# A pool of their own for the small statistics tiles: the same program at other SBUF addresses

## The chip, the cores and the metric

The kernel runs on one core of one Trainium2 chip. The metric is the device time of one execution in microseconds (us). A core has TensorE (PE), which multiplies; VectorE (DVE) and ScalarE (ACT), which work element by element; GpSimd (POOL); SyncE (SP), which here issues nearly all transfers; and DMA engines, which move data between HBM and the on-chip memory, SBUF. A tile in SBUF takes the same byte addresses in each of 128 partitions; "address" below is the byte offset within a partition.

## What is computed

Two layers of a transformer-like trunk for one sequence of 256 tokens with 1,024 features, in fp32. Each layer is a SwiGLU FFN, a mixer, and another FFN, each behind an RMS norm that is modulated by a conditioning vector `c`:

```
mod = (silu(c) @ ada_w[i] + ada_b[i]).reshape(B, 3, 3, 1024)       # shift, scale, gate of each sublayer
pre(z, j) = rms_norm(z, norm_g[i, j]) * (1 + scale[j]) + shift[j]
x = x + 0.5 * gate[0] * swiglu_ffn(pre(x, 0), w_in[i, 0], w_out[i, 0])   # 1024 -> 2 x 2816 -> 1024
x = x + gate[1] * mixer(pre(x, 1))      # layer 0: causal attention, 16 heads; layer 1: convolution module
x = x + 0.5 * gate[2] * swiglu_ffn(pre(x, 2), w_in[i, 1], w_out[i, 1])
```

With 256 tokens the attention has one block, so it is plain causal attention with distance penalties and RMS norms of queries and keys. The convolution module is a pointwise product with a sigmoid gate, a depthwise convolution of width 31, a layer norm, swish and a second pointwise product.

## The kernel before

**Products in three passes.** To come near fp32 accuracy each operand is split into a high part and a low part (the rest), both in the type fp32r. `mm3` (L604) then issues three matmuls for each block: high x high (L606), high x low (L607), low x high (L608). In the trace's names `whi`, `wlo` are the parts of a weight, `hh`, `hl` those of the activations, `gh`, `gl` those of the FFN's hidden values. "u<-whi,hh" is a matmul into the PSUM tile `u` whose moving operand is `whi` (512 columns, 2,048 bytes) and whose stationary operand is 128 columns of `hh`.

**The stream of weights.** `plan` lists all weights in the order of use, in units of 1 MB. `issue` (L187) loads half a unit into one of six `raw` buffers of 4,096 bytes a partition, `high_part` (L229) copies it to `whi` on ScalarE (L241), `step` (L204) makes `wlo` on VectorE (L216). `whi` and `wlo` have six buffers each. Woven into the stream are parts of `ada_w`, which VectorE folds into an accumulator `acc` (`ada_fold`, L279) and TensorE sums over the partitions. The order of all instructions is written out by hand, and the feeding is tied to the products: before each block of products (`block`, L254) a set number of stream entries is taken.

**An FFN** (`ffn`, L641) goes over 11 blocks of 256 hidden columns. For each block and each of two token tiles `cols512` (L610) makes the up-projection into a bank `u` with `hh`/`hl` as stationary operands; `gate` makes `g` (L654, L655); `TR` (L678) transposes `g` (L684) and splits it into `gh` (ACT, L692) and `gl` (DVE, L693); `rows256` (L621), called by `Dn` (L695), makes the down-projection into two banks `y` with `gh`/`gl` as stationary operands. Attention and convolution use the same `rows256` for their last product, with `hh`/`hl` as stationary operands.

**Between sublayers** `residual` (L533) adds to `x`, `square` sums squares into `ss`, and `rms` (L557) makes `v` and `r` from it, one value for each token; `scaled` makes the normalised rows `z`, and `turn` transposes and modulates them (`hf`) into `hh`, `hl`.

**Where tiles lie.** SBUF is given out pool by pool in the order in which pools are opened, within a pool tag by tag as tiles are first asked for. A tile takes a multiple of 32 bytes and begins right behind the last one:

```
self.const = pool("const")
self.rawp = pool("rawp", RAW)
self.hlp = pool("hlp", RING)
self.keep = pool("keep")
self.two = pool("two", 2)
```

`const` holds tables of many sizes and ends at byte 21,088, which is 608 past a multiple of 2,048. `rawp`, `hlp` (`whi`, `wlo`) and `keep` (`x`, `hh`, `hl`) follow with tiles of whole multiples of 2,048 bytes, so all of these begin 608 past a multiple. In `two` the tiles `ss0`, `ss1`, `v0`, `r0`, `v1`, `r1` (4 or 8 bytes, two buffers each) stand between the large ones, so `sq` begins 736, `z` 864, `hf` 992 past a multiple. Each stage then opens a pool of its own (`f0`, `at`, `f1`, `cv`, `f3`) behind `two`: `g`, `gh`, `gl`, `ah`, `al` of the FFNs begin 992 past a multiple. `raw` lies at 21,088 and up, `whi` at 45,664, `wlo` at 94,816, `hh` at 152,160, `hl` at 160,352, `gh` at 203,744 and `gl` at 209,888 (three buffers each).

Of the kernel before, what the change touches and what calls it, by code (L numbers as in the profile page):

```python
# [8 lines left out]
F32 = mybir.dt.float32  # L9
# [25 lines left out]
class Unit:  # L35
    """One megabyte of weights, [128, 2048], as a high and a low part.

    parts: (sources, view of the unit that they fill) twice, half a megabyte each.
    """

# [6 lines left out]
class Vec:  # L47
    """A modulation vector: 0 shift, 1 scale, 2 gate."""

# [7 lines left out]
class Trunk:  # L57
    def __init__(self, ctx, tc, a):
        self.tc, self.nc, self.a = tc, tc.nc, a

        def pool(name, bufs=1, **kw):
            return ctx.enter_context(tc.tile_pool(name=name, bufs=bufs, **kw))

        self.const = pool("const")
        self.rawp = pool("rawp", RAW)
        self.hlp = pool("hlp", RING)
        self.keep = pool("keep")
        self.two = pool("two", 2)
        self.ps = pool("ps", 1, space=bass.MemoryType.PSUM)
        self.vecs = {(l, s, k): Vec(l, s, k) for l in range(2) for s in range(3) for k in range(3)}  # L70
        self.sums = []
        self.phase = 0
        self.ss, self.rs, self.zs = {}, {}, {}
        self.quota = self.credit = 0
        self.plan()

# [1 line left out]
    def plan(self):  # L78
# [3 lines left out]
        def pair_unit(w, c0, n, u):  # L82
            """columns c0.. and c0 + width.. (n of each) of 1024 / n k tiles"""
            nk = 1024 // n
# [5 lines left out]
        def early_unit(w, c0, u):  # L90
            """the same, but with half of the k tiles in each part"""
            rows = w[u * 512 : (u + 1) * 512, :].rearrange("(k p) n -> p k n", p=P)
            return Unit([
                ([rows[:, 2 * s : 2 * s + 2, c : c + 256] for c in (c0, c0 + DFF)], half(s)) for s in range(2)
            ])
# [4 lines left out]
        def col_unit(w, c0, u):  # L100
            """512 columns of four k tiles"""
            rows = w[u * 512 : (u + 1) * 512, c0 : c0 + 512].rearrange("(k p) n -> p k n", p=P)
            return Unit([([rows[:, 2 * s : 2 * s + 2, :]], half(s)) for s in range(2)])

        def row_unit(w, j):
            """all columns of two k tiles"""
            rows = w[j * 256 : (j + 1) * 256, :].rearrange("(k p) n -> p k n", p=P)
# [14 lines left out]
        def weave(main, entries, start):  # L122
            """main units, the entries spread evenly among them from unit number start on"""
            done = 0
# [60 lines left out]

# [1 line left out]
    def issue(self):  # L187
# [16 lines left out]
    def step(self, eng=None):  # L204
        """Take the next entry of the stream; False where it has to wait for a ring slot."""
        nc = self.nc
# [22 lines left out]
    def high_part(self, i):  # L229
        """The high part of entry i; False where it has to wait for a ring slot."""  # L230
        e = self.stream[i]
# [22 lines left out]
    def block(self):  # L254
        """Before a block of products: entries that the other engines can take meanwhile."""
        self.run_sums()
# [49 lines left out]
    def row_sum(self, vec, ah, al, c):  # L306
        """A gate's 512 columns, on all partitions."""
        nc = self.nc
# [6 lines left out]
    def column_sum(self, vec, acc, c):  # L315
        """Four blocks of a shift or a scale, features on the partitions."""
        nc = self.nc
# [5 lines left out]
    def finish(self, vec, src, c, n=4):  # L323
        """Adds the bias; a scale becomes norm_g * (1 + scale)."""
        nc = self.nc
# [9 lines left out]

# [1 line left out]
    def start(self):  # L337
# [53 lines left out]
        def idle(n):  # L391
            """keeps the tensor engine's clock up while it waits"""
            for _ in range(n):
# [5 lines left out]
        nc.tensor.transpose(pt[:, P : P + 72], ab[0], self.ident[:72, :72])  # L399
        self.ss[0] = self.two.tile([P, 2], F32, name="ss0", tag="ss0")  # L400
        self.ss[1] = self.two.tile([P, 2], F32, name="ss1", tag="ss1")
        up = self.p[0]["up"]
# [15 lines left out]
        def turn(q, fold):  # L418
            """The modulation of a quarter and its part of the stationary operand, among the splits."""
            fin = self.early_sum(q, *fold, idle)  # L420
# [23 lines left out]
        def lead(U):  # L444
            """Quarters of the features: their modulation, then three column blocks' products."""
            for q in range(4):
# [15 lines left out]
    def early_fold(self, q):  # L462
        """256 columns of the first scale and shift from four entries of the stream: the vector engine
        folds the scale's two and the shift's first."""
        nc = self.nc
# [21 lines left out]
    def early_sum(self, q, accs, last, idle):  # L487
        """The tensor engine adds the shift's second entry and sums the partitions."""
        nc = self.nc
# [17 lines left out]
    def early_transposes(self, q):  # L507
        """Two k tiles of the normalised rows, features on the partitions."""
        ps = self.bank("m")
# [7 lines left out]
    def early_turn(self, q, ps):  # L517
        """Their modulation; the function that it returns makes them a stationary operand."""
        nc = self.nc
# [11 lines left out]

# [1 line left out]
    def residual(self, t, y, gate, f, last=False):  # L533
        nc, x = self.nc, self.x[t]
        if not last:
            self.ss[t] = self.two.tile([P, 2], F32, name=f"ss{t}", tag=f"ss{t}")
        for o, n in ((0, 512), (512, 256), (768, 256)) if last else ((0, 512), (512, 512)):
# [19 lines left out]
    def rms(self, t, halves=(0, 1)):  # L557
        nc, ss = self.nc, self.ss[t]
        v = self.two.tile([P, 1], F32, name=f"v{t}", tag=f"v{t}")
        r = self.rs[t] = self.two.tile([P, 1], F32, name=f"r{t}", tag=f"r{t}")  # L560
        nc.vector.scalar_tensor_tensor(v, ss[:, 0:1], EPS * D, ss[:, 1:2], op0=ALU.add, op1=ALU.add)
# [4 lines left out]
    def scaled(self, t, h):  # L566
        """512 columns of the normalised rows"""
        z = self.zs[t, h] = self.two.tile([P, 512], F32, name="z", tag="z", bufs=3)
# [4 lines left out]
    def turn(self, t, l, s):  # L573
        """Transposes of the normalised rows, modulated, split into the stationary operand."""
        hf = [self.modulate(t, l, s, h) for h in range(2)]
# [26 lines left out]

# [1 line left out]
    def mm3(self, out, lh, ll, rh, rl, start, stop):  # L604
# [5 lines left out]
    def cols512(self, ps, t, unit, u):  # L610
        """ps [128 tok, 512] += h[t] @ the four k tiles of a unit"""
        self.need(unit)
# [8 lines left out]
    def rows256(self, y, lh, ll, unit, first, last, mid=None):  # L621
        """y (two halves) [128 tok, 1024] += the two k tiles of a unit; lh(k), ll(k): stationary;
        mid(): something to do between the halves"""
        self.need(unit)
# [14 lines left out]

# [1 line left out]
    def ffn(self, i, l, s, before, after, first=None, last=False, mid=None):  # L641
        """before(): turns the second token tile; after(): turns the first for the next sublayer;
        mid(): something to do on the way"""
        nc, p = self.nc, self.p[i]
# [97 lines left out]

# [1 line left out]
    def attention_constants(self):  # L744
        """dist[p, j] = 128 + p - j, or a large number where the key comes after the query. The scores
        are taken over minus the head's slope, so that all heads add the same distances; gqk[., pair]
        carries that and 1 / sqrt(64)."""
        nc = self.nc
# [167 lines left out]

# [1 line left out]
    def taps(self):  # L918
        """w2[32 q + c, r, b] = tap 4 r + q of channel 32 b + c, 0 for tap 31"""
        nc = self.nc  # L920
# [21 lines left out]
    def conv(self, cp, before, after):  # L942
# [35 lines left out]
        def UT(ps, b, t):  # L978
            """ps [128 tok, 256]: both halves of a unit's columns for one token tile"""
            unit = self.pw1[b]  # L980
# [13 lines left out]
        def across(b, t, e, c):  # L994
            """a unit's columns back into the form of U"""
            if b not in us:
# [15 lines left out]
        def spread(b):  # L1012
            """R[32 j + c, g, n] = u[32 g + c, n + j]"""
            u = ub[b % 3]
# [144 lines left out]

# [1 line left out]
    def run(self):  # L1161
# [52 lines left out]
```

## Time and profile before

| | |
|---|---|
| time, median of 3 runs | 1077.59 us (1076.84 to 1079.13) |
| span of the profiled execution, first to last instruction | 1075.8 us |
| what lies around the span, against the median | 1.8 us |
| PE / DVE / ACT busy share of the span | 97% / 76% / 47% |
| granted TensorE clock, mean | 0.984 |
| moved by DMA | 250.26 MB, 233 GB/s in the mean |

The page gives the busy time of each engine, the chain of work that ended last, the costliest groups of instructions and the transfers. A matmul's recorded length is longer than the distance to the next one's start, since matmuls overlap; so the distance of starts is what a product costs, and the recorded length is used to compare alike products. The stages lie at about 0 to 205 us (first FFN), 205 to 375 (attention), 375 to 548 (second FFN), 548 to 722 (third), 722 to 890 (convolution), 890 to 1076 (fourth).

### The profile page before, as it was taken

To read this page: it belongs to the slowest core of one execution; us is meant where nothing else is said; L and a number is where in the kernel's file an instruction comes from. 1 tells how busy PE (TensorE), PEld (TensorE's weight loads), DVE (VectorE), ACT (ScalarE), POOL (GpSimd) and SP (SyncE) were. 2 spreads that over 40 slices of the span, in tenths; PEclk is the share of its full clock that TensorE was granted. 3 is DMA by queue.
4 is the path that set the end of the run, shared out by engine and by line. 5 is a ranking of instruction groups with operands and counts; after the bars stand their busy time and mean duration, and the time that the engine had idled before them with its cause. 6 is when DMAs were issued, how large, how long until landed. Compare 5 with 4: busy or idle time off the path is not lost.

```text
span 1075.8 us, 14807 instructions
## 1 busy us (share of the span) xinstructions
PE 1043.1 (97%) x5522; PEld 853.2 (79%) x5522; DVE 815.4 (76%) x1267; ACT 503.9 (47%) x794; POOL 53.0 (5%) x83
## 2 busy tenths in 40 slices
PE   8999999999999999999999999999988799999998
PEld 7888788877777788888878888888867588888886
DVE  5878878879997798778478788776789768556643
ACT  3354344555676544444354444454545446434420
POOL 3000000001210000000020000000211100000000
PEclk8999999999999999999999999999989899999999
DMA  9979999948766399898739889885646127775711
GB/s 301 295 246 337 300 324 300 328 157 272 235 217 214 115 313 314 282 307 288 240 101 309 287 287 316 283 281 156 172 149 208 61 75 240 262 230 194 232 40 39
DMA packets 181692, 250.26 MB, mean 233 GB/s; under 512 B 8389, under 2 KB 132070, under 8 KB 181620
## 3 DMA queue, kind: packets, MB, share of 16 engines
q1 hardware_dynamic: 180784, 248.55, 70.0%
q0 software_dynamic: 688, 0.71, 0.3%
q8 instruction: 43, 0.70, 0.3%
q14 instruction: 29, 0.24, 0.1%
q10 hardware_dynamic: 148, 0.06, 0.0%
HBM read 248.24 MB, written 1.05 MB: 232 GB/s over the span
## 4 chain that ended last, share of the span: by engine, by line
PE 85%; DVE 9%; issue 2%; DMA 1%; ACT 1%; POOL 1%; SPq 0%; DVEq 0%; POOLq 0%; ACTq 0%
PE u L606 14%; PE u L608 14%; PE u L607 14%; PE y L606 11%; PE y L608 11%; PE y L607 11%; DVE R L1022 3%; DVE wlo L216 2%; PE m L684 2%; PE m L320 1%; DMA raw<-in_ada_w_dram 1%; PE m L497 1%; PE m L1031 1%; DVE x L543 1%; PE m L585 1%
## 5 line engine op out<-in xcount | busy, mean ns | idle before, releaser
L241 ACT ACTIVATE whi<-raw 128x1024 fp32r<-128x1024 f32 x320 | 328.8, 1055 | 167.8 <-DMA raw<-in_ffn_w_in_dram 101.7
L216 DVE TENSOR_TENSOR wlo<-raw,whi 128x1024 fp32r<-128x1024 f32 x320 | 382.5, 1224 | 32.7 <-ACT whi L241 32.6
L606 PE MATMUL u<-whi,hh 128*128 128x512 f32 x672 | 266.5, 397 | 0.0
L608 PE MATMUL u<-whi,hl 128*128 128x512 f32 x672 | 262.8, 391 | 0.0
L607 PE MATMUL u<-wlo,hh 128*128 128x512 f32 x672 | 261.9, 390 | 0.0
L279 DVE SCALAR_TENSOR_TENSOR acc<-raw,sc,acc 128x512 f32<-128x512 f32 x224 | 169.6, 757 | 5.3 <-DMA raw<-in_ada_w_dram 0.4
L608 PEld LDWEIGHTS u<-whi,hl 128*128 128x128 f32 x672 | 126.1, 188 | 28.3 <-DVE hl L601 1.2
L606 PEld LDWEIGHTS u<-whi,hh 128*128 128x128 f32 x672 | 126.3, 188 | 25.7 <-ACT hh L600 0.7
L607 PEld LDWEIGHTS u<-wlo,hh 128*128 128x128 f32 x672 | 126.3, 188 | 25.3
L606 PE MATMUL y<-whi,gh 128*128 128x512 f32 x352 | 140.6, 400 | 0.2 <-ACT gh L692 0.2
L608 PE MATMUL y<-whi,gl 128*128 128x512 f32 x352 | 139.0, 395 | 0.0
L607 PE MATMUL y<-wlo,gh 128*128 128x512 f32 x352 | 138.9, 395 | 0.0
L693 DVE TENSOR_TENSOR gl<-m,gh 128x512 fp32r<-128x512 f32 (+1 forms) x48 | 31.1, 647 | 96.2 <-ACT gh L692 96.0
L606 PE MATMUL y<-whi,hh 128*128 128x512 f32 (+1 forms) x256 | 97.9, 383 | 0.0
L608 PE MATMUL y<-whi,hl 128*128 128x512 f32 (+1 forms) x256 | 95.2, 372 | 0.0
L607 PE MATMUL y<-wlo,hh 128*128 128x512 f32 (+1 forms) x256 | 94.8, 370 | 0.0
L692 ACT ACTIVATE gh<-m 128x512 fp32r<-128x512 f32 (+1 forms) x48 | 26.9, 561 | 135.4 <-PE m L684 135.3
L654 ACT ACTIVATE sg<-u 128x256 f32<-128x256 f32 x84 | 32.2, 383 | 113.3 <-PE u L608 112.3
L608 PEld LDWEIGHTS y<-whi,gl 128*128 128x128 f32 x352 | 66.3, 188 | 16.1 <-DVE gl L693 0.4
L606 PEld LDWEIGHTS y<-whi,gh 128*128 128x128 f32 x352 | 66.3, 188 | 15.2 <-ACT gh L692 0.7
L607 PEld LDWEIGHTS y<-wlo,gh 128*128 128x128 f32 x352 | 66.5, 189 | 14.7
L655 DVE TENSOR_TENSOR g<-u,sg 128x256 f32<-128x256 f32 x84 | 35.5, 422 | 35.0 <-ACT sg L654 34.6
(157 smaller groups left out, 981.0 us busy)
## 6 DMA issues: line engine op xcount, KB each, us to landing
raw<-in_ffn_w_in_dram SPq DMA_DIRECT2D x164, 512.0 KB, 5.2
raw<-in_ada_w_dram SPq DMA_DIRECT2D x144, 512.0 KB, 5.1
raw<-in_ffn_w_out_dram SPq DMA_DIRECT2D x88, 512.0 KB, 5.3
raw<-in_attn_w_qkv_dram SPq DMA_DIRECT2D x24, 512.0 KB, 5.1
raw<-in_conv_w_pw_dram SPq DMA_DIRECT2D x24, 512.0 KB, 5.4
raw<-in_ffn_w_in_dram SPq DMA_DIRECT2D x24, 256.0 KB, 5.5
raw<-in_attn_w_o_dram SPq DMA_DIRECT2D x8, 512.0 KB, 4.4
gate<-in_ada_b_dram SPq DMA_DIRECT2D x6, 512.0 KB, 7.0
```

Of the source, the lines that this page charges most:

```text
L216: (eng or nc.vector).tensor_tensor(lo, raw, hi.bitcast(F32), op=ALU.subtract)
L241: self.nc.scalar.activation(hi, self.like(self.raws[i], hi), AF.Copy)
L279: nc.vector.scalar_tensor_tensor(dst, raw[:, i, :], self.sc[:, k : k + 1], dst, op0=ALU.mult, op1=ALU.add)
L606: nc.tensor.matmul(out, lh, rh, start=start, stop=False)
L607: nc.tensor.matmul(out, lh, rl, start=False, stop=False)
L608: nc.tensor.matmul(out, ll, rh, start=False, stop=stop)
L654: nc.scalar.activation(sg, ps[:, 0:256], AF.Silu)
L655: nc.vector.tensor_tensor(gs[c][:, t, :], ps[:, 256:512], sg, op=ALU.mult)
L684: nc.tensor.transpose(ps[:, o : o + P], g[:, t, k * P : k * P + P], self.ident)
L692: nc.scalar.activation(hi, src, AF.Copy)
L693: nc.vector.tensor_tensor(lo, src, hi.bitcast(F32), op=ALU.subtract)
L1022: nc.vector.tensor_copy(dst, src)
```

## The change

The tiles `ss0`, `ss1`, `v0`, `v1`, `r0`, `r1` get a pool of their own, `tiny`, behind `const`, and a pool with one tile of 264 floats, which nothing reads or writes, fills the bytes up to the next multiple of 2,048. (Comments and docstrings were emptied as well, which moves line numbers by two and nothing else.)

```
         self.const = pool("const")
+        self.tiny = pool("tiny", 2)
+        pool("pad").tile([P, 264], F32, name="pad")
         self.rawp = pool("rawp", RAW)
...
-        self.ss[0] = self.two.tile([P, 2], F32, name="ss0", tag="ss0")
-        self.ss[1] = self.two.tile([P, 2], F32, name="ss1", tag="ss1")
+        self.ss[0] = self.tiny.tile([P, 2], F32, name="ss0", tag="ss0")
+        self.ss[1] = self.tiny.tile([P, 2], F32, name="ss1", tag="ss1")
...
-            self.ss[t] = self.two.tile([P, 2], F32, name=f"ss{t}", tag=f"ss{t}")
+            self.ss[t] = self.tiny.tile([P, 2], F32, name=f"ss{t}", tag=f"ss{t}")
...
-        v = self.two.tile([P, 1], F32, name=f"v{t}", tag=f"v{t}")
-        r = self.rs[t] = self.two.tile([P, 1], F32, name=f"r{t}", tag=f"r{t}")
+        v = self.tiny.tile([P, 1], F32, name=f"v{t}", tag=f"v{t}")
+        r = self.rs[t] = self.tiny.tile([P, 1], F32, name=f"r{t}", tag=f"r{t}")
```

The instructions, their order and the semaphores on which they wait are the same on every engine. What differs is where tiles begin, in bytes past a multiple of 2,048:

| tiles | before | after |
|---|---|---|
| `raw`, `whi`, `wlo`, `x`, `hh`, `hl` | 608 | 0 |
| `sq` | 736 | 0 |
| `z` | 864 | 0 |
| `hf`, the gates, `tmp` | 992 | 0 |
| FFN pools: `g`, `gh`, `gl`, `acc`, `ah`, `al` | 992 | 0 |
| attention pool: `acc`, `vt`, `qT`, `kT` | 1,120 | 128 |
| attention pool: `p` (three buffers of 1,536 bytes) | 1,120, 608, 96 | 128, 1,664, 1,152 |
| convolution pool: `acc`, `b2`, `wd` | 512 | 1,568 |
| convolution pool: `R` (two buffers) | 512, 960 | 1,568, 2,016 |
| `ident`, `ones` and the rest of `const` | as they are | the same |

Behind `const` everything lies 1,056 to 1,440 bytes higher: `hh` at 153,600, `gh` at 204,800.

## Rows read from the trace of the kernel before

**Rows 1.** The page: busy times, and the chain's shares by engine.

```profile
PE 1043.1 (97%) x5522; PEld 853.2 (79%) x5522; DVE 815.4 (76%) x1267; ACT 503.9 (47%) x794; POOL 53.0 (5%) x83
...
PE 85%; DVE 9%; issue 2%; DMA 1%; ACT 1%; POOL 1%; SPq 0%; DVEq 0%; POOLq 0%; ACTq 0%
```

**Rows 2.** Stretches: PE, PEld, DVE, ACT, POOL busy us (count); clock, DMA share, GB/s.

```profile
60.00:205.00 145.00, 144.78 (x666) 118.71 (x665) 122.28 (x162) 65.43 (x84) 0.00 (x0) 1.00 0.90 304
375.00:548.00 173.00, 171.80 (x798) 141.59 (x797) 131.19 (x172) 73.92 (x94) 0.55 (x1) 1.00 0.83 277
...
892.00:1062.00 170.00, 170.00 (x762) 139.01 (x761) 98.46 (x117) 70.30 (x92) 0.00 (x0) 1.00 0.57 188
```

**Rows 3.** Timeline of PE, an up-projection (start, length).

```profile
928.84 0.39 PE L606 MATMUL u<-whi,hh 128*128 128x512 f32 x1
...
933.37 0.40 PE L608 MATMUL u<-whi,hl 128*128 128x512 f32 x1
```

**Rows 4.** Timeline of PE, a down-projection, its first product and the next block's.

```profile
1042.24 0.40 PE L606 MATMUL y<-whi,gh 128*128 128x512 f32 x1
...
1047.83 0.39 PE L606 MATMUL u<-whi,hh 128*128 128x512 f32 x1
```

**Rows 5.** By tile (hh, gh, gl): min/median/max of each product's record.

```profile
L606 PE MATMUL u<-whi,hh x672: 387/389/501, 22.0 to 1064.4; 128*128 128x512 f32 x168
...
L606 PE MATMUL y<-whi,gh x352: 390/395/498, 74.4 to 1070.2; 128*128 128x512 f32 x176
...
L607 PE MATMUL y<-wlo,gh x352: 390/393/404, 74.7 to 1070.4; 128*128 128x512 f32 x176
...
L608 PE MATMUL y<-whi,gl x352: 388/393/499, 74.9 to 1070.6; 128*128 128x512 f32 x176
```

**Rows 6.** Groups of PE's instructions by form: busy, mean ns.

```profile
L606 PE MATMUL u<-whi,hh 128*128 128x512 f32 x672 | 266.5, 397 | 0.0
...
L607 PE MATMUL u<-wlo,hh 128*128 128x512 f32 x672 | 261.9, 390 | 0.0
L606 PE MATMUL y<-whi,gh 128*128 128x512 f32 x352 | 140.6, 400 | 0.2 <-ACT gh L692 0.2
...
L607 PE MATMUL y<-wlo,gh 128*128 128x512 f32 x352 | 138.9, 395 | 0.0
L606 PE MATMUL y<-whi,hh 128*128 128x512 f32 x192 | 79.7, 415 | 0.0
```

**Rows 7.** The same groups, 867.3 to 875.3 us (the convolution's last product).

```profile
L607 PE MATMUL y<-wlo,hh 128*128 128x512 f32 x13 | 5.1, 389 | 0.0
```

**Rows 8.** Timeline of PE behind an interruption, 864.2 to 867.5 us.

```profile
864.95 0.40 PE L607 MATMUL y<-wlo,hh 128*128 128x512 f32 x1
...
867.49 0.39 PE L606 MATMUL y<-whi,hh 128*128 128x512 f32 x1
```

**Rows 9.** What ACT waited for in the first FFN, 60 to 205 us.

```profile
ACT whi L241 <- DMA raw<-in_ffn_w_in_dram: 18.8, 9, 6.3
```

**Rows 10.** Line 279 in the attention and the convolution: min/median/max.

```profile
L279 DVE SCALAR_TENSOR_TENSOR acc<-raw,sc,acc x25: 740/751/753, 251.0 to 316.7; 128x512 f32<-128x512 f32 x25
...
L279 DVE SCALAR_TENSOR_TENSOR acc<-raw,sc,acc x14: 744/752/2396, 761.3 to 816.3; 128x512 f32<-128x512 f32 x14
```

**Rows 11.** By tile (ident, p): transposes of g, z and p: min/median/max.

```profile
L684 PE MATMUL m<-ident,g x176: 270/272/330, 68.1 to 1066.6; 128*128 128x128 f32 x176
...
L585 PE MATMUL m<-ident,z x80: 270/272/303, 226.7 to 890.9; 128*128 128x128 f32 x80
...
L853 PE MATMUL m<-ident,p x48: 270/272/328, 270.2 to 340.5; 128*128 128x128 f32 x48
```

**Rows 12.** DMA issues: KB each, median us from issue to landing.

```profile
raw<-in_ffn_w_out_dram SPq DMA_DIRECT2D x88, 512.0 KB, 5.3
...
raw<-in_attn_w_o_dram SPq DMA_DIRECT2D x8, 512.0 KB, 4.4
...
b<-in_conv_b_pw_dram POOLq DMA_DIRECT2D x1, 512.0 KB, 4.7
```

## The prediction

> **What bounds the kernel now.** I read the page's busy line first: TensorE is busy 97% of a span of 1075.8 us, VectorE 76%, ScalarE 47% [rows 1]. A busy PE is not a PE at its peak, so the next view is the busy table by stage. In the first, second and fourth FFN stretches (the third is like the second) PE is busy 486.6 of 488 us at a granted clock of 1.00, while the DMA share is 0.90, 0.83 and 0.57, and VectorE is idle for 23, 42 and 72 us of them [rows 2]. So there the time is the number of products times the step from one product's start to the next's, and nothing else. Outside of them other engines have a part: of the chain that ended last PE is 85%, VectorE 9%, DMA 1% [rows 1].
>
> Then the step itself. In a run of up-projection products (L606 to L608, stationary `hh`/`hl`, moving `whi`/`wlo`, 512 columns) the starts at 928.84 and 933.37 us are 20 products apart: 226.5 ns each [rows 3]. In a run of down-projection products, same lines, same shapes, stationary `gh`/`gl`, the starts at 1042.24 and 1047.83 us are 24 products apart: 232.9 ns each [rows 4]. The recorded lengths agree (a record is longer than a step, because products overlap): median 389 ns with `hh`, 395 and 393 with `gh`, 393 with `gl` [rows 5]; the means of L606 and L607 are 397 and 390 against 400 and 395 [rows 6]. It is not the form of the down-projection: the convolution's last product has the same two-k-tile form and writes the same `y` banks, but its stationary operand is `hh`, and from 867.3 to 875.3 us its mean is 389 [rows 7]. It is hardly a wait either: L606 and L607 with `gh` have 0.2 us of idle time before them in all [rows 6]. After an interruption products with `hh` step unevenly too, for a while: soon behind transposes the 11 steps from 864.95 to 867.49 us take 230.9 ns each [rows 8]; then comes the 389 that was just named. Those with `gh` never get there. What distinguishes `gh` and `gl` is where they lie.
>
> **The change, part by part.**
> *What it moves.* Nothing is added or removed: every engine has the same instructions in the same order with the same semaphore waits. Only byte addresses change. The weights' buffers, `x`, `hh` and `hl` go from 608 past a multiple of 2,048 bytes to 0; `z` from 864 to 0; `gh`, `gl`, `g`, `hf`, the gates from 992 to 0. So the moving operand and `hh` move together, as they stood together before, and `gh`, which stood 384 bytes further on in its 2 KB than the moving operand, now stands at the same place.
>
> *The down-projection's products* are the term of the sum: 352 x 3 = 1,056 [rows 6]. If their uneven step comes from that difference of 384 bytes, they fall into the step of `hh`, which has the same relation before and after. The gain of one is 4.0 ns by the means ((3 + 5) / 2) [rows 6], 4.7 ns by the medians ((6 + 4 + 4) / 3, 389 taken for each `hh`) [rows 5], 6.4 ns by the two runs of starts [rows 3, 4]: 4.2, 4.9 or 6.8 us in all. The means of `hh` contain its own uneven stretches after transposes, which the down-projection, coming straight after products, mostly doesn't have; so I take a value nearer to the runs, 5.6 ns, 5.9 us. A quarter of these products lie in the first FFN. There the DMA share is 0.90 [rows 2] and ScalarE waits 18.8 us for the up-projection's weights alone [rows 9]; a faster PE meets later weights, and I let half of that quarter, 0.7 us, be lost. In the other three FFNs what covers the feeding is the DMA share of 0.83 and below and VectorE's spare time; if that cover were gone, their 4.4 us would be lost as well. Sum: 5.2 us.
>
> *VectorE and ScalarE* get nothing. The accumulator of L279 already stands at different distances from the `raw` that it is read with: 1,120 past a multiple in the attention pool, 512 in the convolution's, `raw` at 608. Its medians are 751 and 752 ns [rows 10]. The split at L216 reads and writes tiles that all stand at 608 and will all stand at 0. I cost these edits at nothing.
>
> *Transposes and the convolution's fp32 products* get nothing. A transpose takes 272 ns with `z` (864), `g` (992) and `p` (1,120, 608 or 96 past a multiple) alike [rows 11]. Bound: 4.7 ns, the difference between `gh` and `hh`, on these 304 would be 1.4 us in either direction; I take 0.
>
> *DMAs.* `raw` stood 608 past a multiple of 2,048, so 96 past a multiple of 256. `b2`, at 512, is a multiple of 256 already: its 512 KB landed 4.7 us after issue, between the 4.4 of `attn_w_o` and the 5.3 of `ffn_w_out` into `raw`, rows of the same 4 KB [rows 12]. I take nothing. Bound: 1% of the chain is DMA [rows 1], 10.8 us; from 5.3 down to 4.7, 11%, would be 1.2 us.
> The Trainium skill (DMA: Bandwidth & Descriptors, How a descriptor splits into AXI transactions) says that a descriptor that doesn't begin at a multiple of 256 B pays beats for the bytes in front. By it a 1 KB piece would go from 35 beats to 32, an estimate from that page; on the chain's 1% that is about 0.9 us, so the sum would be 6.1 instead of 5.2 us. The trace doesn't bear it out: `b2`, which pays no such beats, landed no sooner than `attn_w_o`, which would.
>
> *Sum against the time.* The profiled span is 1075.8 us, 1.8 below the median of the runs, 1077.6; that remainder stays. 1075.8 - 5.2 + 1.8 = **1072.4 us**, 0.5% faster. What a measurement of this kernel can tell from no change is about 0.2%, 2.2 us.
>
> **The rivals.**
> *No change: the place within 2 KB is not the cause* (1077.6 us, 1075.5 to 1079.5). `gh` and `gl` differ from `hh` in a second way: they are the only stationary operands of the three-pass products that lie above byte 200,000 of a partition (`hh` at 152,000, weights below 144,000), and they stay there. For it speaks that all four pieces of a `gh` tile, which stand at 992, 1,504, 2,016 and 480, step unevenly, whereas the four of `hh` at 608, 1,120, 1,632 and 96 all run evenly: shifts by 512 bytes make no difference, so only some of the possible relations are left. Against it: `p` above byte 212,000 is transposed in the same 272 ns as `z` at 171,000 [rows 11]. The trace of before cannot separate the two, since no such operand lies high at the good place or low at the bad one.
> A rule speaks for this rival too: the Trainium skill (SBUF — State Buffer, Who interferes with whom) says that PE has two independent read ports and never waits on anyone. By that rule no placement changes a step and the time stays 1077.6; the two runs of starts, 226.5 and 232.9 ns on the same lines, show that something on the operand's side does matter.
>
> *Slower: the absolute place decides, and 0 is a bad one.* Nothing in the trace stands at 0 past a multiple of 2,048 and feeds TensorE. If `hh` and the moving weights lose their even step there as `gh` has none now, the 672 x 3 + 192 x 3 = 2,592 products of 512 columns with `hh` [rows 6] pay the same 5.6 ns: 14.5 us, about 1092 us with `gh` unimproved. It decides the sign once `hh` loses more than 2.0 ns a product (5.2 us / 2,592). Half of that effect would be 1085. Against it: `hh` is even at 608, 1,120, 1,632 and 96, some of which cross a multiple of 2,048 and some not; a start exactly at one should be no worse.
>
> *Faster still*: the landing price above (1.2 us) and the even step returning sooner after transposes. The mean of L606 lies 7 ns above that of L607 [rows 6], much of it behind interruptions; 672 x 7 ns is 4.7 us, and if 0.6 of it went, 2.8 us were saved: about 1068.4 with both.
>
> **How the numbers follow.** The even step for `gh`: 0.50. Faster still, on top of it: 0.05. No change: 0.31, since a second cause is as simple and the rule says so. Slower: 0.14, for an untried place. The likeliest case alone spans 1070.8 (6.8 us, nothing lost) to 1073.9 (4.2 us by the means, half of the first FFN's quarter lost). The range takes that and the no-change case and leaves out most of the two ends: 1069.5 to 1080.5. Faster by over 0.2% (below 1075.4): 0.54; within 0.2%: 0.31; slower: 0.15, the hundredth added for small losses.
>
> **What would show it.** Right: products with `gh` at a median of 389 and 24 starts of a down-projection 5.44 us apart instead of 5.59; L216, L279 and the transposes as before; the first FFN gaining less than the others. Wrong: `gh` still at 393 to 395 (then place within 2 KB is not the cause); products with `hh` above 389 (the slower rival); landings of `raw` in L201 clearly under 5.3 us for `ffn_w_out` (the DMA rule); or an even `gh` whose gain turns up as PE waits for weights.

## The result, and the profile after

Five runs of the changed kernel took 1070.13 to 1072.88 us, median 1071.31, against a median of 1077.59 before. The ratio is 0.9942 with a 95% interval from 0.9930 to 0.9954: 0.58% faster, 6.3 us. 1072.4 us was forecast, within a range from 1069.5 to 1080.5.

Line numbers of the changed kernel are two higher: L608 to L610 are the three passes. The page of its profiled execution, which was the slowest of the five, against [rows 1]:

```profile
PE 1038.3 (97%) x5522; PEld 853.5 (80%) x5522; DVE 815.1 (76%) x1267; ACT 503.8 (47%) x794; POOL 53.2 (5%) x83
...
PE 87%; DVE 8%; issue 2%; ACT 1%; DMA 1%; POOL 1%; SPq 0%; DVEq 0%; POOLq 0%; ACTq 0%
```

PE is as busy as before, 97%, but for 4.8 us less; the busy times of the other engines, and of the weight loads, are the same within 0.5 us. So all of the 4.8 us by which the profiled span is shorter are busy time of TensorE. Which products it came out of, the timeline of PE shows in the fourth FFN, at the same products as [rows 3, 4]: the last product with `hl`, the first with `gh`, and the first of the next up-projection:

```profile
1037.62 0.39 PE L610 MATMUL u<-whi,hl 128*128 128x512 f32 x1
1037.85 0.39 PE L608 MATMUL y<-whi,gh 128*128 128x512 f32 x1
1038.08 0.39 PE L609 MATMUL y<-wlo,gh 128*128 128x512 f32 x1
...
1043.06 0.39 PE L610 MATMUL y<-whi,gl 128*128 128x512 f32 x1
1043.29 0.39 PE L608 MATMUL u<-whi,hh 128*128 128x512 f32 x1
```

The 24 products with `gh` and `gl` now take from 1037.85 to 1043.29 us, 5.44 us or 226.7 ns each, where they took 5.59 us. That is the step of the up-projection, and it is there from the first product on. By tile (min/median/max of a record), against [rows 5]:

```profile
L608 PE MATMUL y<-whi,gh x352: 387/389/497, 74.5 to 1065.4; 128*128 128x512 f32 x176
...
L609 PE MATMUL y<-wlo,gh x352: 387/389/398, 74.8 to 1065.6; 128*128 128x512 f32 x176
```

```profile
L610 PE MATMUL y<-whi,gl x352: 387/389/496, 75.0 to 1065.8; 128*128 128x512 f32 x176
```

And the groups of PE by form (busy, mean ns), against [rows 6] and the row of `gl` before:

```profile
L608 PE MATMUL y<-whi,gl 128*128 128x512 f32 x352 | 139.0, 395 | 0.0
```

```profile
L608 PE MATMUL u<-whi,hh 128*128 128x512 f32 x672 | 266.5, 397 | 0.0
...
L609 PE MATMUL u<-wlo,hh 128*128 128x512 f32 x672 | 261.8, 390 | 0.0
L608 PE MATMUL y<-whi,gh 128*128 128x512 f32 x352 | 138.8, 394 | 0.2 <-ACT gh L694 0.2
L610 PE MATMUL y<-whi,gl 128*128 128x512 f32 x352 | 137.3, 390 | 0.0
L609 PE MATMUL y<-wlo,gh 128*128 128x512 f32 x352 | 137.1, 389 | 0.0
```

With `hh` nothing has changed (397 and 390 as before), with `gh` and `gl` the medians fell from 395, 393 and 393 to 389. The busy times of the three groups with `gh` and `gl` fell from 140.6, 139.0 and 138.9 to 138.8, 137.3 and 137.1 us: by 5.3 us together, or 5.0 ns a product.

How much of it becomes time is seen by FFN. Of the products with `wlo` and `gh` the rows below give the first and the last start in the first, the second and the fourth FFN, before:

```profile
L607 PE MATMUL y<-wlo,gh x88: 390/395/404, 74.7 to 229.9; 128*128 128x512 f32 x88
...
L607 PE MATMUL y<-wlo,gh x88: 390/393/404, 378.6 to 550.8; 128*128 128x512 f32 x88
...
L607 PE MATMUL y<-wlo,gh x88: 390/393/404, 905.8 to 1070.4; 128*128 128x512 f32 x88
```

and after:

```profile
L609 PE MATMUL y<-wlo,gh x88: 387/389/397, 74.8 to 229.0; 128*128 128x512 f32 x88
...
L609 PE MATMUL y<-wlo,gh x88: 387/389/396, 378.4 to 549.6; 128*128 128x512 f32 x88
...
L609 PE MATMUL y<-wlo,gh x88: 389/389/395, 902.7 to 1065.6; 128*128 128x512 f32 x88
```

By the starts to a hundredth the stretch shrank from 155.19 to 154.14 us in the first FFN, from 172.21 to 171.15 in the second, from 171.66 to 170.29 in the third and from 164.56 to 162.92 in the fourth: by 1.05, 1.06, 1.37 and 1.64, 5.1 us in all. This repeats: in all seven profiled executions with `gh` at the even step (below) the four stretches are 154.0 to 154.1, 171.0 to 171.2, 170.0 to 170.3 and 162.8 to 162.9 us. What lies between the FFNs varies from execution to execution: in the same seven the attention, from the last such start of the first FFN to the first of the second, is 148.2 to 149.5 us long, and the convolution, between the third and the fourth, 156.8 to 159.0. So 5.1 us is what the trace shows to be the change's, and the 1.2 us more between the medians can't be told from that variation.

One such difference is in the pair of profiles itself: the execution after has a piece at half clock in the attention (granted clock 0.50 from 247 to 249 us), which that of before has not. The busy table of 240 to 256 us before, after, and in another execution of the changed kernel (the run `e_again` below; the clock is the third number from the end):

```profile
240.00:256.00 16.00, 13.80 (x63) 10.91 (x62) 13.71 (x23) 8.61 (x16) 2.42 (x1) 1.00 0.72 223
```

```profile
240.00:256.00 16.00, 13.81 (x56) 10.90 (x55) 13.03 (x20) 7.69 (x13) 2.58 (x2) 0.89 0.73 231
```

```profile
240.00:256.00 16.00, 13.78 (x63) 10.90 (x62) 14.69 (x20) 8.26 (x13) 4.53 (x2) 1.00 0.80 254
```

About the same 13.8 us of PE hold 63 instructions before and 56 after, at a granted clock of 1.00 and 0.89. Seven instructions fewer are about 1.7 us lost (13.8 x 7 / 56, an estimate that takes the instructions as alike); measured, the attention takes 149.45 us there and 148.16 in the other execution of the same kernel, whose clock stayed at 1.00. So the piece does not come with the change as such.

### The profile page after: what moved, and what is told of

The parts are those of the page before. It is cut to its first block, busy times and chain, and to the rows that moved or that the text cites. A ratio compares the mean times of both kernels' runs of the same rounds, so it can differ in the third digit from the quotient of the medians.

```text
span 1071.0 us, 14807 instructions
## 1 busy us (share of the span) xinstructions
PE 1038.3 (97%) x5522; PEld 853.5 (80%) x5522; DVE 815.1 (76%) x1267; ACT 503.8 (47%) x794; POOL 53.2 (5%) x83
## 3 DMA queue, kind: packets, MB, share of 16 engines
HBM read 248.24 MB, written 1.05 MB: 233 GB/s over the span
## 4 chain that ended last, share of the span: by engine, by line
PE 87%; DVE 8%; issue 2%; ACT 1%; DMA 1%; POOL 1%; SPq 0%; DVEq 0%; POOLq 0%; ACTq 0%
PE u L608 15%; PE u L610 15%; PE u L609 14%; PE y L608 11%; PE y L610 11%; PE y L609 11%; DVE R L1024 2%; DVE wlo L218 2%; PE m L686 2%; PE m L322 1%; PE m L1033 1%; DMA raw<-in_ada_w_dram 1%; PE m L499 1%; DVE x L545 1%; PE m L587 1%
## 5 line engine op out<-in xcount | busy, mean ns | idle before, releaser
L608 PE MATMUL u<-whi,hh 128*128 128x512 f32 x672 | 266.5, 397 | 0.0
L610 PE MATMUL u<-whi,hl 128*128 128x512 f32 x672 | 262.7, 391 | 0.0
L281 DVE SCALAR_TENSOR_TENSOR acc<-raw,sc,acc 128x512 f32<-128x512 f32 x224 | 169.5, 757 | 5.6 <-DMA raw<-in_ada_w_dram 0.7
L610 PEld LDWEIGHTS u<-whi,hl 128*128 128x128 f32 x672 | 126.1, 188 | 28.4 <-DVE hl L603 1.2
L608 PEld LDWEIGHTS u<-whi,hh 128*128 128x128 f32 x672 | 126.3, 188 | 25.5 <-ACT hh L602 0.6
L608 PE MATMUL y<-whi,gh 128*128 128x512 f32 x352 | 138.8, 394 | 0.2 <-ACT gh L694 0.2
L610 PE MATMUL y<-whi,gl 128*128 128x512 f32 x352 | 137.3, 390 | 0.0
L609 PE MATMUL y<-wlo,gh 128*128 128x512 f32 x352 | 137.1, 389 | 0.0
L608 PE MATMUL y<-whi,hh 128*128 128x512 f32 (+1 forms) x256 | 98.2, 384 | 0.0
L610 PE MATMUL y<-whi,hl 128*128 128x512 f32 (+1 forms) x256 | 94.7, 370 | 0.0
L610 PEld LDWEIGHTS y<-whi,gl 128*128 128x128 f32 x352 | 66.1, 188 | 14.6 <-DVE gl L695 0.4
L608 PEld LDWEIGHTS y<-whi,gh 128*128 128x128 f32 x352 | 66.1, 188 | 13.8 <-ACT gh L694 0.7
```

Source lines behind the costliest of these rows:

```text
L281: nc.vector.scalar_tensor_tensor(dst, raw[:, i, :], self.sc[:, k : k + 1], dst, op0=ALU.mult, op1=ALU.add)
L608: nc.tensor.matmul(out, lh, rh, start=start, stop=False)
L609: nc.tensor.matmul(out, lh, rl, start=False, stop=False)
L610: nc.tensor.matmul(out, ll, rh, start=False, stop=stop)
```

## The experiments

All of them change only where tiles lie; the instructions stay the same. A distance below is that of a stationary operand's tile from the moving operand's, in bytes, each taken within its 2,048. "Changed" is the kernel after the change. Ratios are to runs of the kernel before on the same chip.

**`gh` brought to the weights' place, and nothing else.** The kernel before with one line:

```
         self.two = pool("two", 2)
+        pool("pad").tile([P, 416], F32, name="pad")
```

> The kernel before, with a filler of 1,664 bytes behind the pool of z and hf alone: weights and hh stay 608 past a multiple of 2,048, gh and gl go from 992 to 608 as well, so that they stand where the moving operand stands. If the relation of stationary and moving operand decides: products with gh at a median of 389 ns, 1071 to 1073 us, nearly all of the change's gain. If a start at a multiple of 2,048 is needed (for TensorE or for the DMAs): gh at 393 to 395, 1077 to 1078 us.

1072.03 us, ratio to the kernel before 0.9954 (0.9942 to 0.9967). By tile:

```profile
L608 PE MATMUL y<-wlo,gh x352: 387/389/398, 75.5 to 1065.1; 128*128 128x512 f32 x176
```

No tile of the products begins at a multiple of 2,048 here, and 389 is there and so is the time. The multiples are not needed.

**`gh` taken away again, all else aligned.** The changed kernel with a filler:

```
         self.two = pool("two", 2)
+        pool("pad2").tile([P, 96], F32, name="pad2")
```

> The changed kernel, with a filler of 384 bytes in front of the stages' pools: weights, x, hh, z stay at multiples of 2,048; gh, gl, g go to 384 past one, the distance that they had before. Relation theory: gh back at 393 to 395, 1076 to 1078 us. If the rest of the alignment (weights, raw, x at multiples) brought the gain: 1071 to 1073 us.

1079.0 us, ratio 1.001 (1.0002 to 1.0019), 1 us above the expectation's range: the whole gain is gone.

```profile
L610 PE MATMUL y<-wlo,gh x352: 387/393/405, 75.4 to 1072.1; 128*128 128x512 f32 x176
```

**Everything at the place that `gh` had.** The changed kernel with a larger filler:

```
-        pool("pad").tile([P, 264], F32, name="pad")
+        pool("pad").tile([P, 512], F32, name="pad")
```

> The changed kernel with the filler at 2,048 bytes instead of 1,056, so that all large tiles begin 992 past a multiple of 2,048, where gh stood before, together with the weights and hh. Relation theory: gh and hh at 389, 1070 to 1073 us. Absolute place theory (992 is a bad start): gh and hh both at 393 to 395, about 1090 us. If the DMAs gain from starts at multiples of 256: landings of raw back from 5.0 to 5.2 us, and 1 us more than the changed kernel at most.

1072.3 us, ratio 0.9951 (0.9938 to 0.9963). By tile, with `hh` and with `gh`, and two of the DMA issues (KB each, median us to landing):

```profile
L609 PE MATMUL u<-wlo,hh x672: 386/389/399, 23.8 to 1059.3; 128*128 128x512 f32 x168
...
L609 PE MATMUL y<-wlo,gh x352: 387/389/397, 76.3 to 1065.0; 128*128 128x512 f32 x176
```

```profile
raw<-in_ffn_w_out_dram SPq DMA_DIRECT2D x88, 512.0 KB, 5.3
...
raw<-in_attn_w_o_dram SPq DMA_DIRECT2D x8, 512.0 KB, 4.5
```

992 past a multiple is no bad place when the moving operand stands there too: the absolute place falls, the relation stands. The landing of `ffn_w_out` is 5.3 us, as before the change; in the changed kernel it is 5.1 (below). That is not the alignment's doing: in the kernel of the experiment above, where `raw` stands at the same addresses as in the changed one, it is 5.4:

```profile
raw<-in_ffn_w_out_dram SPq DMA_DIRECT2D x88, 512.0 KB, 5.4
```

The time of this kernel and that of the changed one are not told apart.

**All stationary operands moved away from the moving ones.** The changed kernel with a filler between the weights and `x`, `hh`, `hl`:

```
+        pool("pad2").tile([P, 96], F32, name="pad2")
         self.keep = pool("keep")
```

> The changed kernel, with a filler of 384 bytes between the weights' pools and x, hh, hl: now hh, hl and gh, gl all stand 384 bytes further on in their 2 KB than the moving weights. Relation theory: all 3,648 products of 512 columns step unevenly, hh and gh at 393 to 395, 5.2 ns more each: 1071.3 + 19 = 1090 us, 1084 to 1092. If it is something of gh alone (its height in the partition, how it is written): hh at 389, 1071 to 1078 us.

1087.15 us, ratio 1.0088 (1.0072 to 1.0103), 15.8 us more than the changed kernel's 1071.31. By tile:

```profile
L609 PE MATMUL u<-whi,hh x672: 389/393/482, 23.0 to 1074.2; 128*128 128x512 f32 x168
L610 PE MATMUL u<-wlo,hh x672: 387/393/405, 23.2 to 1074.4; 128*128 128x512 f32 x168
...
L610 PE MATMUL y<-wlo,hh x256: 274/393/632, 26.0 to 889.4; 128*128 128x512 f32 x96, 128*128 128x256 f32 x32
L609 PE MATMUL u<-hh,whi x64: 279/282/583, 790.6 to 833.8; 128*128 128x256 f32 x64
```

`hh` now has the 393 that `gh` had: it is nothing of `gh` alone. The medians account for it: 4 ns on 2,592 products with `hh` are 10.4 us and the 4.9 of `gh` [rows 5] make 15.3; the expectation had taken 5.2 ns for each. The convolution's products of 256 columns, in which the weights are the stationary operand (last row: median 282 ns, before and after 283), lost nothing when the two operands stood 384 apart.

One rival is left by the placing: the buffers of `raw` always stand where the weights stand, so the loads and splits of weights could be what disturbs a product, and not its own moving operand. The trace of before settles it. The run of [rows 4] with 232.9 ns a step lies behind the last load and split; in its time the DMA share is 0.01, and VectorE and ScalarE have one instruction each:

```profile
1042.20:1047.90 5.70, 5.70 (x26) 4.60 (x25) 0.42 (x1) 0.39 (x1) 0.00 (x0) 1.00 0.01 3
```

The uneven step needs none of the feeding: what is left at work are TensorE's own two operands.

**Which distances.** Three kernels, each the changed one with a filler of its own size in front of the FFN pools, here for 32 bytes in the first:

```
-        with tc.tile_pool(name="f0", bufs=1) as self.fp:
+        with tc.tile_pool(name="pf0", bufs=1) as pad, tc.tile_pool(name="f0", bufs=1) as self.fp:
+            pad.tile([P, 8], F32, name="padf0")
```

> The changed kernel with fillers in front of the FFN pools, so that gh and gl stand 32 bytes (first FFN), 64 bytes (second and third) and 128 bytes (fourth) further on in their 2 KB than the moving weights. If any distance that is not a multiple of 512 spoils the even step: gh at 393 to 395 in all three stretches. If it takes a larger distance: gh at 389 in the first ones.

> The same with 192, 256 and 320 bytes. If any distance that is no multiple of 512 spoils the step: 393 to 395 in all. If the relation repeats every 256 bytes: 389 in the second and third FFN (256), 393 to 395 in the others.

> The same with 448, 480 and 512 bytes. Pieces of hh 512 bytes apart all step evenly, so 512 (fourth FFN) gives 389; 448 and 480 give 393 to 395 if any other distance spoils the step.

The products with `wlo` and `gh` by tile, in the first FFN, the second and third, the fourth; first 32, 64 and 128 bytes:

```profile
L609 PE MATMUL y<-wlo,gh x71: 392/395/403, 75.6 to 204.5; 128*128 128x512 f32 x71
...
L609 PE MATMUL y<-wlo,gh x156: 392/398/398, 380.0 to 719.8; 128*128 128x512 f32 x156
...
L609 PE MATMUL y<-wlo,gh x77: 390/395/404, 907.8 to 1061.9; 128*128 128x512 f32 x77
```

then 192, 256 and 320:

```profile
L609 PE MATMUL y<-wlo,gh x72: 388/394/398, 75.1 to 203.9; 128*128 128x512 f32 x72
...
L609 PE MATMUL y<-wlo,gh x160: 387/389/398, 379.2 to 718.8; 128*128 128x512 f32 x160
...
L609 PE MATMUL y<-wlo,gh x80: 393/396/398, 903.2 to 1059.6; 128*128 128x512 f32 x80
```

then 448, 480 and 512:

```profile
L609 PE MATMUL y<-wlo,gh x72: 388/394/398, 74.8 to 203.6; 128*128 128x512 f32 x72
...
L609 PE MATMUL y<-wlo,gh x159: 390/396/398, 378.2 to 719.6; 128*128 128x512 f32 x159
...
L609 PE MATMUL y<-wlo,gh x80: 389/389/389, 905.1 to 1059.6; 128*128 128x512 f32 x80
```

Medians of 395, 398, 395, 394, **389**, 396, 394, 396 and **389**: the even step is there at 0, 256 and 512, and at none of the other distances run between them (the 398 at 64 lies above the 393 to 395 that were expected). 192 and 448 are alike (394), as are 64 and 320 within 2 ns; so, as far as these distances tell, it repeats every 256 bytes. The relation needs a multiple of 256, not of 512, as the expectation for 512 left open.

The starts say the same, and that the bad distances are not all equally bad. Taking the down-projection's products that come more than 12 products behind an interruption (transposes or sums), the mean step is 226.6 to 226.8 ns at 256 and 512, 232.8 to 233.3 at 32, 64, 128, 320 and 480, but 229.1 and 229.2 at 192 and 448. Each of the three kernels ran once: 1079.8 us with all four FFNs at a bad distance, 1075.4 with two (one of them at 192) and 1075.25 with three (one of them at 448).

**The smallest filler that does it.** The kernel before, 384 bytes behind `two`, which makes the distance 768:

```
         self.two = pool("two", 2)
+        pool("pad").tile([P, 96], F32, name="pad")
```

> The kernel before with one line more: a filler of 384 bytes behind the pool of z and hf. No tile that is at a multiple of 2,048 after the change is at one here (weights and hh 608, gh and gl 1,376 past one), but gh now stands 768 bytes, three times 256, further on in its 2 KB than the moving operand. If the relation repeats every 256 bytes, as the scan says: gh at 389, 1071 to 1073 us. If it needs 512 or the scan misled: 393 to 395 and 1077 us.

1071.88 us, ratio 0.9944 (0.9930 to 0.9958), beside the changed kernel on the same chip with 0.9945 (`e_again`, below). By tile:

```profile
L608 PE MATMUL y<-wlo,gh x352: 387/389/398, 74.8 to 1065.0; 128*128 128x512 f32 x176
```

**The constants of the transposes aligned as well.** `ident` and `ones` in a pool of their own, everything else 1,024 past a multiple:

```
+        self.sq128 = pool("sq128")
...
-        self.ident = const.tile([P, P], F32, name="ident")
+        self.ident = self.sq128.tile([P, P], F32, name="ident")
```

> The changed kernel with ident and ones, the constant operands of transposes and sums, moved out of the constants' pool to 0 and 512 past a multiple of 2,048, and all large tiles at 1,024 past one. If the uneven steps of hh behind transposes come from ident's and ones' distance to the other operands: the mean of u<-whi,hh falls from 397 towards 392 and the time by 1 to 4 us, to 1067 to 1070. If they come from the interruption itself: 397, and 1070 to 1073 us.

1069.52 us, ratio 0.9923 (0.9911 to 0.9935), but the groups by form show no reason for it:

```profile
L609 PE MATMUL u<-whi,hh 128*128 128x512 f32 x672 | 266.3, 396 | 0.0
...
L610 PE MATMUL u<-wlo,hh 128*128 128x512 f32 x672 | 261.9, 390 | 0.0
```

396 and 390 for `hh` as against 397 and 390. So it was run again, beside the changed kernel:

> The kernel with ident and ones aligned once more. Its products step as those of the changed kernel, so it should be the same within 1 us, 1070 to 1072; if the 1069.5 of its first run was no accident of the chip or the clock, 1.5 to 2 us less than the changed kernel beside it.

> The changed kernel once more, beside the next one on the same chip: 1071 to 1072 us.

1071.46 us (0.9942, 0.9929 to 0.9954) against 1071.69 (0.9945, 0.9931 to 0.9958): the same. The first result did not repeat. Of the 2.9 us by which the spans of its two profiled executions differ (1067.5 and 1070.4), 1.75 lie in the convolution (156.77 and 158.52 us) and none in the four FFN stretches, which agree within 0.02 us. The theory that the uneven steps behind transposes come from these constants' place falls.

## Why the prediction was right

*The bound.* That the FFNs are bound by the step of PE's products held: a change of 5 to 6 ns in the step of a part of them came through in the time.

*The term of the sum.* 5.6 ns on 1,056 products, 5.9 us, less 0.7 us lost in the first FFN, 5.2 us in all was forecast. The four FFN stretches give 5.1, the recorded lengths 5.3, the medians of the time 6.3 with an interval from 5.0 to 7.5 us (0.9954 and 0.9930 of 1077.59). That the number is so close is in part luck, for two errors cancel. An undisturbed product gained more than was taken: 6.2 ns by the two runs of 24 (232.9 and 226.7), which on all 1,056 would be 6.5 us. And 1.4 us of that did not come, twice the 0.7, for another reason and not in the first FFN alone: the second gained as little, 1.06 us, and the third 1.37 of a possible 1.6.

What the prediction had wrong there is the wait. A faster PE met no later weights: from the first to the last start in the rows above, the steps of the up-projection's products take 82.45 us before and 82.51 after in the first FFN, 99.54 and 99.58 in the second. The gain is missing in the down-projection itself. In the first three FFNs transposes and the sums of `ada_w` stand between its products, and the prediction's "mostly" was too much: of its products (some 250 in each FFN whose step can be read) 84, 65 and 52 come within 12 products behind such an interruption, in the fourth only 14. In the first FFN the first four behind an interruption went from 233.4 to 231.6 ns a step, the next eight from 233.3 to 230.0, all later ones from 232.6 to 226.8. Besides, PE's wait for the last `g` at the end of each of the first three FFNs grew by some 0.14 us (in the first from 1.20 to 1.35 us of idle time). These two make up most of the 1.4 us; for the rest the traces show no reason.

*The cause.* The distance between stationary and moving operand was named, as the first of two explanations that the trace could not separate. Four runs separate them: `gh` joined to the weights gives the gain without any alignment, `gh` taken 384 bytes away loses it, everything at 992 keeps it, and `hh` taken away loses about as much for each product (4 ns by the medians) as `gh` had lost. What the prediction left open is the period. It saw that shifts by 512 don't matter and stopped there; 256 is enough, so the change's multiples of 2,048 are more than is needed.

*The rivals.* No change: `gh` is still above byte 200,000 and now even, so its height is not the cause. The Trainium skill's rule that weighed for this rival (SBUF — State Buffer, Who interferes with whom) has PE's two read ports as independent, and PE as waiting on no one. The first doesn't hold here to the last few ns: with the same instructions and waits 4 to 6 ns of a product come and go with the place of one operand against the other. The second is not touched by it: the 232.9 ns are there with hardly another engine at work. Slower, because 0 is a bad place: `hh` is at 389 with a start at 0 as with 608 and 992, and `gh` with starts at 256, 512 and 1,376 too. Faster still: the mean of L608 with `hh`, which contains the steps behind interruptions, is unchanged, 397. The landings, against [rows 12]:

```profile
raw<-in_ffn_w_out_dram SPq DMA_DIRECT2D x88, 512.0 KB, 5.1
...
raw<-in_attn_w_o_dram SPq DMA_DIRECT2D x8, 512.0 KB, 4.6
...
b<-in_conv_b_pw_dram POOLq DMA_DIRECT2D x1, 512.0 KB, 4.3
```

`ffn_w_out` 5.1 after 5.3, `b2` 4.3 after 4.7, `attn_w_o` 4.6 after 4.4. By the Trainium skill's rule (DMA: Bandwidth & Descriptors, How a descriptor splits into AXI transactions) a descriptor that starts at a multiple of 256 pays fewer beats, so the rows of `raw` should land sooner. `attn_w_o` didn't; `b2` landed sooner though it now starts 1,568 past a multiple of 2,048, 32 off a multiple of 256, and was at one before; and `ffn_w_out` took 5.4 us in the experiment above with `raw` aligned as here. So these differences show nothing of the rule.

*What was costed at nothing.* The fold of L281 in the attention stage, against [rows 10], and the transposes, against [rows 11], stand as they did (medians of 751 and 272 ns before):

```profile
L281 DVE SCALAR_TENSOR_TENSOR acc<-raw,sc,acc x28: 740/752/754, 244.6 to 316.5; 128x512 f32<-128x512 f32 x28
```

```profile
L686 PE MATMUL m<-ident,g x176: 270/272/332, 68.2 to 1061.9; 128*128 128x128 f32 x176
L587 PE MATMUL m<-ident,z x80: 270/272/300, 225.8 to 887.8; 128*128 128x128 f32 x80
L855 PE MATMUL m<-ident,p x48: 271/273/329, 270.2 to 340.4; 128*128 128x128 f32 x48
```

Open are two things. Why a distance that is no multiple of 256 makes the step uneven is not shown: the runs show the relation, its period and its price. And the uneven steps behind an interruption, of some ten products, are there before and after the change and were not explained.

## What to carry to other kernels

Where PE is the bound, compare the record's length of like products by their tiles: two groups with the same form and no waits that differ by one or two per cent can point at where the operands lie. In this kernel products of 512 columns keep the even step when the stationary operand begins a multiple of 256 bytes away from the moving one; a single filler of 384 bytes in front of the right pool brings all of it, and small tiles that stand between large ones in a pool are what had spoilt it. A saving for each product is worked out stage by stage: here products that follow an interruption closely gained only a part of it. A result that the profile gives no reason for is run again before it is believed.

## What had not been expected of the hardware

The placement of SBUF operands shows in TensorE's step. With 512 columns of fp32r and new weights for each product the step over 24 products is 226.7 ns at a distance of 0 between stationary and moving operand, and 232.9 ns at 384; medians of the record are 389 at distances of 0, 256, 512 and 768 bytes and 393 to 398 at all others that were run. The loss is not spread evenly: in the nine unbroken runs of 24 products with `gh` and `gl` in the fourth FFN before the change, every seventh step (the first, eighth, 15th and 22nd) takes 241 to 242 ns in the mean and nearly all others 230 to 233; after it all 24 take 227. Products of 256 columns did not mind: 282 ns with 384 bytes between the operands, 283 with 0. VectorE's fold into `acc`, 512 columns, took 751 or 752 ns wherever `acc` stood against `raw`: 384, 512 and 1,952 bytes further on before, 0, 128 and 1,568 after.
